# Order of high and low weight products, and the address of the high weights, in a hybrid decoder layer

## The chip, the cores and the metric

One core of one Trainium2 chip runs the whole program in one launch. The metric is device time in microseconds, from the start to the end of the execution, lower is better. The core has five instruction streams that run side by side and wait for each other by semaphores: TensorE (matmuls, PE in the profile, with PEld for the loads of its stationary operand), VectorE (DVE), ScalarE (ACT), GpSimd (POOL) and SyncE (SP, which here only issues DMAs).

## The reference

One decoder layer on 256 tokens of width 2048, in fp32. The weights are read once, 241 MB in all, and almost all the work lies in products of the 256 token rows with them:

```python
h = rms_norm(x, pre_mix_norm[l])
gq, gk, gv, gz, ga, gb, mq, mk, mv = jnp.split(h @ w_in[l], split_at, axis=-1)
y_gdn = gdn_branch(gq, gk, gv, gz, ga, gb, conv_w[l], a_log[l], dt_bias[l], gdn_norm_w[l])
y_moba = moba_branch(mq, mk, mv)
mix = jnp.concatenate([y_gdn, y_moba], axis=-1) @ w_out[l]
x = x + rms_norm(mix, post_mix_norm[l])
ca = memory_cross_attention(rms_norm(x, pre_mem_norm[l]), rms_norm(mem, mem_kv_norm[l]),
                            w_mq[l], w_mk[l], w_mv[l], w_mo[l])
x = x + rms_norm(ca, post_mem_norm[l])
f = jnp.square(jax.nn.relu(rms_norm(x, pre_mlp_norm[l]) @ w_up[l])) @ w_down[l]
x = x + rms_norm(f, post_mlp_norm[l])
```

`gdn_branch` is a gated delta rule over chunks with 8 heads, after a short convolution; `moba_branch` is causal softmax attention with 8 heads (at 256 tokens there is only the own block).

## The kernel before

**Three products for one.** TensorE works on operands of the type fp32r. To keep fp32's accuracy the kernel splits each operand into a high part, rounded to that type, and a low part, the rest. A product is then high x high + high x low + low x high, summed in one PSUM bank.

**The stream of weights.** `Stream` brings the weights in units of 128 x 1024 elements (128 x 512 for the first four), each by one DMA on SyncE's queue into a buffer `wraw` (5 of them). ScalarE casts it to `whi` (4 buffers) and VectorE subtracts to get `wlo` (4 buffers). `next()` hands out the next unit and issues those up to three ahead. `plan` lists the units in the order of use.

**Two kinds of products.** In the transposed ones (`a_tile`, `a_group`) the weights are the stationary operand and the tokens stream, so that the result has its features on the partitions. An activation tile holds high and low side by side (2 x 256 columns, `act[2][k]`), so the high weights take one matmul of 512 columns and the low weights one of 256 columns on the high half (`act[0][k]`). `a_tile` makes one tile of 128 features in 16 steps over the model width, two units of 8 steps; `a_group` makes four such tiles at once, in units of two steps by four tiles. `products` issues for each unit first its eight high matmuls and then its eight low ones (four and four in the first four units). In the other kind (`b_group`) the activation is stationary and the weights stream, 512 columns at a time, three matmuls for each step. Its last group in the cross-attention's output and in the layer's end splits the second of its two tiles into halves of 256 columns: for each unit six matmuls of 512 and then twelve of 256.

**The order of the work.** TensorE's order is that of the code (`manual_schedule`). After each unit `tick()` advances generators in the list `bg`, which hold the small work of the mixer and of the norms (transposes, Gram matrices, softmax); their matmuls stand between units. The other engines' order is made by the scheduler from the program's dependences; `pin` holds a few in place. Stages in time: the input projection with the mixer (activation `x`, to about 410 us), the output projection, the cross-attention (activations `m` and `h1`), and from about 597 us the MLP (activation `h`), twice half of the up projection (transposed) and half of the down projection (`b_group`, activations `f` and `fp`).

**Names in the rows.** `whi` and `wlo` are the high and low weights. `mm<-h,whi` is a matmul into a bank `mm` with moving `h` and stationary `whi`; `mm<-whi,fp` has the activation `fp` stationary. `wabh` are the high weights of the small gate projection (40 columns, slices of 160 bytes). Line 49 is `mm`, line 69 the cast, line 71 the subtraction. `mmb`, a broadcast row of the memory's norm, is the tile that changes its pool.

Of the kernel before, what the change touches and what calls it, by code (L numbers as in the profile page):

```python
# [7 lines left out]
F32 = mybir.dt.float32  # L8
F32R = mybir.dt.float32r
# [7 lines left out]
P = 128  # L17
T = 256
D = 2048
KT = 16  # L20
H = 8
HM = 4
# [6 lines left out]
NRAW, NHI, NLO, AHEAD = 5, 4, 4, 3  # L29
# [7 lines left out]
def layer(ctx, tc, x0, xT, xn, memT, cols, rows, wab, win, wout, wmq, wmk, wmv, wmo, wup, wdn, out):  # L37
# [4 lines left out]
    wp = ctx.enter_context(tc.tile_pool(name="wp", bufs=1))  # L42
    ap_ = ctx.enter_context(tc.tile_pool(name="act", bufs=1))
    sm = ctx.enter_context(tc.tile_pool(name="sm", bufs=1))
# [3 lines left out]
    def mm(o, l, r, start=True, stop=True, skip=False):  # L48
        TE.matmul(o, l, r, start=start, stop=stop, skip_group_check=skip)  # L49
# [3 lines left out]
    class Stream:  # L53


        def __init__(s, plan):
            s.units, s.done, s.pos, s.pin, s.ahead = [], [], 0, 0, AHEAD
            for n, (src, a, fine) in enumerate(plan):
                step = 1 if fine else a // 2
                s.units += [(n, src, a, k, step, fine) for k in range(0, a, step)]  # L60

        def emit(s):
            n, src, a, k, step, fine = s.units[len(s.done)]
            v = src.rearrange("p (a c) -> p a c", a=a)
            c = v.shape[2]
            r = wp.tile([P, step, c], F32, tag="wraw", name="wraw", bufs=NRAW)
            nc.sync.dma_start(r, v[:, k:k + step])
            hi = wp.tile([P, step, c], F32R, tag="whi", name="whi", bufs=NHI)
            cast = S.activation(hi, r, AF.Copy)  # L69
            lo = wp.tile([P, step, c], F32R, tag="wlo", name="wlo", bufs=NLO)  # L70
            sub = V.tensor_tensor(lo, r, hi.bitcast(F32), OP.subtract)  # L71
            if s.pin:
                s.pin -= 1
                pin(cast), pin(sub)
            s.done.append([(hi[:, i], lo[:, i]) for i in range(step)])
# [11 lines left out]
    def tick():  # L87
        for g in list(bg):
            if next(g, bg) is bg:
                bg.remove(g)  # L90
# [5 lines left out]
    def mmps():  # L96
        return ps.tile([P, 512], F32, tag="mm", name="mm", bufs=5)

    def aux():
        return ps.tile([P, 512], F32, tag="ax", name="ax", bufs=3)  # L100

    def products(steps):


        for o, w, act, k, first, last in steps:
            mm(o, w[0], act[2][k], start=first, stop=False)
        for o, w, act, k, first, last in steps:
            mm(o[:, :T], w[1], act[0][k], start=False, stop=last)

    def right(o):  # L110

# [4 lines left out]
    def a_tile(act):  # L116

        o = mmps()
        k = 0
        while k < KT:  # L120
            u = ws.next()
            products([(o, w, act, k + i, k + i == 0, k + i == KT - 1) for i, w in enumerate(u)])
            k += len(u)
            tick()
        return o

    def a_group(act, order, pre=None):

        o = [mmps() for _ in range(4)]
        n = 0  # L130
        while n < KT:
            u = ws.next()
            if pre:
                pre(n)
            cut = lambda w, c: [x[:, c * P:(c + 1) * P] for x in w]
            products([(o[c], cut(w, c), act, order[n + i], n + i == 0, n + i == KT - 1)
                      for i, w in enumerate(u) for c in range(4)])
            n += len(u)
            tick()
        return o  # L140

    def b_group(act, kts, last=False, banks=None):

        o = banks or [mmps() for _ in range(2)]
        whole = [[(b, slice(0, 512))] for b in o]
        if last:
            whole[1] = [(o[1][:, 0:T], slice(0, T)), (mmps()[:, 0:T], slice(T, 512))]

        def run(t, units, k):
            s = slice(t * P, (t + 1) * P)  # L150
            for b, c in whole[t]:
                for i, w in enumerate(units):
                    kt = kts[k + i]
                    f, l = k + i == 0, k + i == len(kts) - 1
                    mm(b, act[0][kt][:, s], w[0][:, c], start=f, stop=False)
                    mm(b, act[0][kt][:, s], w[1][:, c], start=False, stop=False)
                    mm(b, act[1][kt][:, s], w[0][:, c], start=False, stop=l)

        k = 0
        while k < len(kts):  # L160
            w = ws.next()
            while last and len(kts) - 8 <= k < len(kts) - len(w):
                w = w + ws.next()
            for t in range(2):
                run(t, w, k)
            k += len(w)
            tick()
        return whole
# [70 lines left out]
    def xslot(name):  # L239
        return parts(ap_.tile([P, KT, 2, T], F32R, tag="x", name=name))  # L240

    plan = [(win[i], 4, i == 0) for i in range(4)]
    for what, h in TURNS:
        i, n = {"mv": (24 + 4 * h, 4), "kq": (2 * h, 2), "m": (32 + 2 * h, 2), "v": (16 + h, 1), "z": (48 + h, 1)}[what]
        plan += [(win[i + j], 4 if what == "mv" else KT, False) for j in range(n)]
    plan += [(wout[i], 4, False) for i in range(16)]
    plan += [(wmk[i], KT, False) for i in range(HM)]
    plan += [(wmq[i], 4, False) for i in range(HM)]
    plan += [(wmv[i], 4, False) for i in range(4)]
    plan += [(wmo[i], 4, False) for i in range(4)]  # L250
    for half in range(2):
        plan += [(wup[32 * half + i], 4 if half == 0 and i < 4 else KT, False) for i in range(32)]
        plan += [(wdn[32 * half + i], 4, False) for i in range(32)]
    ws = Stream(plan)

    def scaled(dst, o, by, const=1.0):
# [12 lines left out]
    def prep(act, src, wcol, pool, k0, n, sq):  # L269
        xs = pool.tile([P, n, T], F32, tag="xs", name="xs", bufs=2 if n > 2 else 4)  # L270
        k1 = k0 % 4
        nc.sync.dma_start(xs, src[k0 // 4, :, k1:k1 + n])
        for k in range(n):
            norm_split(act, xs[:, k], wcol, k0 + k)
        S.activation(sq[:, k1:k1 + n], xs, AF.Square)

    def fold(sq):
        for n in (2, 1):
            V.tensor_tensor(sq[:, 0:n], sq[:, 0:n], sq[:, n:2 * n], OP.add)

    def col_sum(sq, name):

        pc = aux()
        for t in range(2):
            mm(pc[:, t:t + 1], sq[:, t * P:(t + 1) * P], ones[:, 0:1])
        return rstd_cols(pc[:, 0:2], name)
# [71 lines left out]
    with tc.tile_pool(name="p1", bufs=1) as p1:  # L358
        def t1(shape=None, name="t1"):
            return p1.tile(shape or [P, T], F32, tag="t1", name=name, bufs=14)  # L360
# [266 lines left out]
        mv = p1.tile([P, 2, 1024], F32, name="mv")  # L627
# [77 lines left out]
        for what, h in TURNS:  # L705
            if what == "mv":
                o = b_group(hx, list(range(KT)), banks=[mmps(), mmps() if h else aux()])
# [9 lines left out]
            if what == "m":  # L717
                q, k = t1(), t1()
# [6 lines left out]
            if what == "z":  # L725
                o = a_tile(hx)
# [6 lines left out]
        order = list(range(8, 15)) + list(range(8)) + [15]  # L733
# [6 lines left out]
    with ExitStack() as es:  # L740
        p2 = es.enter_context(tc.tile_pool(name="p2", bufs=1))
# [75 lines left out]
        ssm = []  # L817
        with tc.tile_pool(name="ld2", bufs=1) as ld2:
            def mem_in():
                acc = ld2.tile([P, 4, T], F32, name="macc")  # L820
                for q in range(4):
                    sq = ld2.tile([P, 4, T], F32, tag="msq", name="msq", bufs=2) if q else acc
                    prep(hm, memT, n_kv, ld2, 4 * q, 4, sq)
                    yield
                    if q:
                        V.tensor_tensor(acc, acc, sq, OP.add)
                    yield
                    yield
                fold(acc)
                for q in range(4):  # L830
                    nc.sync.dma_start(x1[:, 4 * q:4 * q + 4], xT[q])
                    yield
                yield
                ssm.append(col_sum(acc[:, 0], "mmr"))
                for _ in range(3):
                    yield
                ssm.append(sm.tile([P, T], F32, tag="mmb", name="mmb"))
                row_bcast(*ssm)

            bg.append(mem_in())  # L840
            late = list(range(12, 16)) + list(range(12))
            for c in range(4):
                om = b_group(y, order) if c else out_first
                stat_out(om, c, mix, lambda d, s: S.activation(d, s, AF.Copy))
            assert not bg
# [48 lines left out]
        o = b_group(hm, list(range(KT)), banks=[mmps(), aux()])  # L894
# [40 lines left out]
        for j in range(8):  # L935
            o = o_first[j] if j < 4 else a_tile(h2)
# [7 lines left out]
    for half in range(2):  # L944
# [11 lines left out]
        for c in range(4):  # L956
            o = b_group(f, list(range(32)), last=half == 1 and c == 3)
            cs = slice(512 * c, 512 * (c + 1))
# [14 lines left out]
    for t in range(2):  # L973
# [5 lines left out]
        for c in range(4):  # L979
            cs = slice(512 * c, 512 * (c + 1))  # L980
# [78 lines left out]
```

## Time and profile before

| | |
|---|---|
| runs (3) | median 1317.57 us, 1316.19 to 1318.88 |
| profiled execution | 1317.31 us, span of the core 1315.5 us |
| granted clock of TensorE, mean | 0.995 |
| TensorE busy with matmuls | 1295.0 us, 98% of the span, 6945 instructions |
| TensorE loading weights (beside the matmuls) | 1115.1 us, 85% |
| VectorE, ScalarE, GpSimd busy | 66%, 51%, 3% |
| DMA | 246 MB, mean 187 GB/s |

Busy time of TensorE is made of overlapping matmuls whose ends are modelled, so 98% says that it hardly ever stands still, not that it works at its peak. How fast it goes is read from the starts of its matmuls.

### The profile page before, as it was taken

The numbers are of one execution on the slowest core, as the hardware profiler recorded it, in microseconds if no ns is written. First come the engines' busy times: TensorE is split into PE (matmuls) and PEld (weight loads), VectorE is DVE, ScalarE is ACT, GpSimd is POOL, SyncE is SP. The second block draws the span as 40 slices with busy tenths as digits, with TensorE's granted clock in tenths as the row PEclk, the third lists the DMA queues.
The fourth block names the chain that finished last, engine by engine and source line by source line (L and its number), as shares of the span: only waits on it lengthen the run. The fifth ranks groups of instructions, "written<-read, shape, count | busy, mean of one in ns | idle before, by whom it ended". The sixth has DMA issues, their size and how long they took to land.

```text
span 1315.5 us, 18643 instructions
## 1 busy us (share of the span) xinstructions
PE 1295.0 (98%) x6945; PEld 1115.1 (85%) x6945; DVE 873.0 (66%) x1528; ACT 664.7 (51%) x1028; POOL 35.4 (3%) x64
## 2 busy tenths in 40 slices
PE   9999999999999999999999999999999999999997
PEld 8888888898887788888888888888888888888886
DVE  8988879867575759759966654444466666554555
ACT  7655544525555757657644444444444444443442
POOL 1010010100000000000000000000000000000000
PEclk9999999999999999999999999999999999999998
DMA  8655565624446865744665656666655565666662
GB/s 308 190 183 182 187 192 172 194 82 144 144 130 224 290 213 169 246 154 145 196 190 191 191 178 195 196 192 195 196 193 189 184 190 191 214 198 193 193 190 86
DMA packets 72378, 246.25 MB, mean 187 GB/s; under 512 B 10408, under 2 KB 11872, under 8 KB 71904
## 3 DMA queue, kind: packets, MB, share of 16 engines
q1 hardware_dynamic: 70016, 239.27, 56.3%
q0 software_dynamic: 2272, 5.80, 1.5%
q8 instruction: 54, 0.88, 0.3%
q14 instruction: 36, 0.29, 0.1%
HBM read 241.35 MB, written 3.69 MB: 186 GB/s over the span
## 4 chain that ended last, share of the span: by engine, by line
PE 66%; DMA 3%; DVE 2%; ACT 1%; issue 1%; DVEq 0%; SPq 0%; ACTq 0%; POOLq 0%
PE mm L49 63%; PE ax L49 2%; DMA xs<-in_memT_dram 2%; DMA t<-rd 1%; DMA wraw<-in_wout_dram 1%; DVE wlo L71 1%; PE ax L778 0%; DVE ca L981 0%; ACT whi L69 0%; DMA rd<-t 0%; ACT m L231 0%; PE ax L886 0%; DVE fd L965 0%; DVE yg L681 0%; ACT ca L772 0%
## 5 line engine op out<-in xcount | busy, mean ns | idle before, releaser
L71 DVE TENSOR_TENSOR wlo<-wraw,whi 128x1024 fp32r<-128x1024 f32 (+1 forms) x434 | 528.1, 1219 | 371.7 <-ACT whi L69 369.6
L69 ACT ACTIVATE whi<-wraw 128x1024 fp32r<-128x1024 f32 (+1 forms) x434 | 456.2, 1054 | 519.2 <-PE mm L49 341.4
L49 PE MATMUL mm<-h,whi 128*128 128x512 f32 x1024 | 256.8, 393 | 0.0
L49 PE MATMUL mm<-whi,fp 128*128 128x512 f32 (+1 forms) x816 | 240.3, 377 | 0.0
L49 PEld LDWEIGHTS mm<-h,whi 128*128 128x128 f32 x1024 | 184.2, 189 | 33.2 <-DVE h L232 0.2
L49 PE MATMUL mm<-x,whi 128*128 128x512 f32 x768 | 201.0, 404 | 1.1 <-ACT whi L69 1.1
L49 PEld LDWEIGHTS mm<-whi,fp 128*128 128x128 f32 x816 | 150.2, 188 | 28.1
L49 PEld LDWEIGHTS mm<-x,whi 128*128 128x128 f32 x768 | 140.7, 191 | 27.6 <-ACT whi L69 1.5
L49 PE MATMUL mm<-wlo,fp 128*128 128x512 f32 (+1 forms) x408 | 153.7, 377 | 0.0
L49 PEld LDWEIGHTS mm<-h,wlo 128*128 128x128 f32 x1024 | 139.7, 190 | 10.0
L49 PE MATMUL mm<-h,wlo 128*128 128x256 f32 x1024 | 142.8, 282 | 0.0
L49 PEld LDWEIGHTS mm<-x,wlo 128*128 128x128 f32 x768 | 105.2, 190 | 8.0
L49 PE MATMUL mm<-x,wlo 128*128 128x256 f32 x768 | 107.4, 282 | 0.0
L49 PEld LDWEIGHTS mm<-wlo,fp 128*128 128x128 f32 x408 | 76.8, 188 | 14.2
L49 PE MATMUL mm<-whi,f 128*128 128x512 f32 (+1 forms) x272 | 81.0, 377 | 0.0
L49 PEld LDWEIGHTS mm<-whi,f 128*128 128x128 f32 x272 | 50.1, 188 | 9.4
L49 PE MATMUL mm<-wlo,f 128*128 128x512 f32 (+1 forms) x136 | 51.3, 377 | 0.0
L113 ACT ACTIVATE right<-mm 128x256 f32<-128x256 f32 x120 | 44.9, 378 | 4.6 <-PE mm L49 2.5
L49 PE MATMUL mm<-whi,ym 128*128 128x512 f32 x128 | 42.5, 393 | 0.9 <-ACT whi L69 0.9
L49 PE MATMUL mm<-whi,yg 128*128 128x512 f32 x128 | 41.9, 391 | 0.4 <-ACT whi L69 0.4
L381 DVE SCALAR_TENSOR_TENSOR t<-xc,cl,t 128x256 f32<-128x256 f32 x72 | 34.6, 481 | 2.6 <-ACT t L379 1.5
L49 PE MATMUL mm<-whi,x 128*128 128x512 f32 x96 | 31.8, 396 | 0.0
(359 smaller groups left out, 1246.8 us busy)
## 6 DMA issues: line engine op xcount, KB each, us to landing
wraw<-in_wup_dram SPq DMA_DIRECT2D x128, 512.0 KB, 3.9
wraw<-in_wdn_dram SPq DMA_DIRECT2D x128, 512.0 KB, 4.4
wraw<-in_win_dram SPq DMA_DIRECT2D x110, 512.0 KB, 4.0
wraw<-in_wout_dram SPq DMA_DIRECT2D x32, 512.0 KB, 5.0
wraw<-in_wmk_dram SPq DMA_DIRECT2D x8, 512.0 KB, 4.5
wraw<-in_wmq_dram SPq DMA_DIRECT2D x8, 512.0 KB, 4.2
wraw<-in_wmv_dram SPq DMA_DIRECT2D x8, 512.0 KB, 5.1
wraw<-in_wmo_dram SPq DMA_DIRECT2D x8, 512.0 KB, 3.7
```

The source lines that it names most:

```text
L49: TE.matmul(o, l, r, start=start, stop=stop, skip_group_check=skip)
L69: cast = S.activation(hi, r, AF.Copy)
L71: sub = V.tensor_tensor(lo, r, hi.bitcast(F32), OP.subtract)
L113: S.activation(t, o[:, T:], AF.Copy)
L381: V.scalar_tensor_tensor(y, c[:, i:i + T], cw[:, 4 * ch + i:4 * ch + i + 1], y, OP.mult, OP.add)
```

## The change

The eight high and eight low matmuls of a unit no longer stand in two blocks: each high one is followed at once by its low one, in `a_tile` and in `a_group`. The tiles `whi` grow from 1024 to 1088 elements per partition. A unit that will be stationary is written 48 elements (192 bytes) into its buffer, one that will stream at the buffer's start. The 1 KB that this takes is given back by moving `mmb` from a pool that lasts all along to one that is opened later.

```diff
             for src, a, fine, off in plan:
                 step = 1 if fine else a // 2
-                s.units += [(n, src, a, k, step, fine) for k in range(0, a, step)]
+                s.units += [(src, a, k, step, off) for k in range(0, a, step)]
...
-            hi = wp.tile([P, step, c], F32R, tag="whi", name="whi", bufs=NHI)
+            hi = wp.tile([P, 1024 + 64], F32R, tag="whi", name="whi", bufs=NHI)
+            hi = hi[:, off:off + step * c].rearrange("p (a c) -> p a c", a=step)
             cast = S.activation(hi, r, AF.Copy)
...
-    def products(steps):
-
-
-        for o, w, act, k, first, last in steps:
-            mm(o, w[0], act[2][k], start=first, stop=False)
-        for o, w, act, k, first, last in steps:
-            mm(o[:, :T], w[1], act[0][k], start=False, stop=last)
+    def three(o, whi, wlo, act, k, first, last):
+
+        mm(o, whi, act[2][k], start=first, stop=False)
+        mm(o[:, :T], wlo, act[0][k], start=False, stop=last)
...
         while k < KT:
-            u = ws.next()
-            products([(o, w, act, k + i, k + i == 0, k + i == KT - 1) for i, w in enumerate(u)])
-            k += len(u)
+            for w in ws.next():
+                three(o, *w, act, k, k == 0, k == KT - 1)
+                k += 1
             tick()
...
-            products([(o[c], cut(w, c), act, order[n + i], n + i == 0, n + i == KT - 1)
-                      for i, w in enumerate(u) for c in range(4)])
-            n += len(u)
+            for w in u:
+                for c in range(4):
+                    cs = slice(c * P, (c + 1) * P)
+                    three(o[c], w[0][:, cs], w[1][:, cs], act, order[n], n == 0, n == KT - 1)
+                n += 1
...
-        plan += [(wup[32 * half + i], 4 if half == 0 and i < 4 else KT, False) for i in range(32)]
-        plan += [(wdn[32 * half + i], 4, False) for i in range(32)]
+        plan += [(wup[32 * half + i], 4 if half == 0 and i < 4 else KT, False, 48) for i in range(32)]
+        plan += [(wdn[32 * half + i], 4, False, 0) for i in range(32)]
...
-                ssm.append(sm.tile([P, T], F32, tag="mmb", name="mmb"))
+                ssm.append(p2.tile([P, T], F32, tag="mmb", name="mmb"))
```

The rest of `plan` gets its offsets in the same way: 48 for the input projection's transposed parts and for `wmk` and `wmq`, 0 for the values (`mv`), `wout`, `wmv` and `wmo`.

On TensorE, at the beginning of the MLP, the order before is this (`ca` is transposed for the norm, `h` is the normed activation):

```order
L778 MATMUL ax<-ident,ca 128x128 x16
L49 MATMUL mm<-h_6036,whi 128x512 x8
L49 MATMUL mm<-h_6036,wlo 128x256 x8
L778 MATMUL ax<-ident,ca 128x128 x4
L49 MATMUL mm<-h_6036,whi 128x512 x8
```

Of the change, at the same place, behind the transposes that stand between two units:

```order
L778 MATMUL ax<-ident,ca 128x128 x4
L49 MATMUL mm<-h_6036,whi 128x512
L49 MATMUL mm<-h_6036,wlo 128x256
L49 MATMUL mm<-h_6036,whi 128x512
L49 MATMUL mm<-h_6036,wlo 128x256
```

The blocks of eight are gone; the transposes stay where they were, between units. All transposed products change in this way, from the first instruction of the input projection on.

On ScalarE, early in the mixer, the order before is this (`right` is the copy of a bank's right half, `x0b` the broadcast norm):

```order
L69 ACTIVATE whi<-wraw 128x1024 x2
L113 ACTIVATE right<-mm 128x256 x2
L69 ACTIVATE whi<-wraw 128x1024 x4
L212 ACTIVATE x0b<-ax 128x256
L113 ACTIVATE right<-mm 128x256 x2
```

And of the change:

```order
L70 ACTIVATE whi<-wraw 128x1024 x3
L111 ACTIVATE right<-mm 128x256 x2
L70 ACTIVATE whi<-wraw 128x1024 x3
L211 ACTIVATE x0b<-ax 128x256
L111 ACTIVATE right<-mm 128x256 x2
```

One cast moved ahead of two copies. ScalarE's and VectorE's instructions change places by a few positions at some places up to the mixer's end, and stand as before behind it. Line numbers shift by one or two with the edit.

## Rows read from the trace of the kernel before

**Rows 1.** The page: busy time of TensorE; its granted clock in 40 slices.

```profile
PE 1295.0 (98%) x6945; PEld 1115.1 (85%) x6945; DVE 873.0 (66%) x1528; ACT 664.7 (51%) x1028; POOL 35.4 (3%) x64
...
PEclk9999999999999999999999999999999999999998
```

**Rows 2.** Groups of TensorE by shape: count, busy us, mean ns of one.

```profile
L49 PE MATMUL mm<-h,whi 128*128 128x512 f32 x1024 | 256.8, 393 | 0.0
...
L49 PE MATMUL mm<-x,whi 128*128 128x512 f32 x768 | 201.0, 404 | 1.1 <-ACT whi L69 1.1
L49 PE MATMUL mm<-h,wlo 128*128 128x256 f32 x1024 | 142.8, 282 | 0.0
...
L49 PE MATMUL ax<-x,wabh 128*40 128x256 f32 x32 | 5.7, 279 | 0.0
```

**Rows 3.** Timeline of TensorE in the MLP: start, length of the merged row, count.

```profile
701.89 2.00 PE L49 MATMUL mm<-h,whi 128*128 128x512 f32 x8
703.73 1.12 PE L49 MATMUL mm<-h,wlo 128*128 128x256 f32 x8
...
710.27 0.40 PE L49 MATMUL mm<-h,whi 128*128 128x512 f32 x1
```

**Rows 4.** Timeline of TensorE, activation-stationary products of the cross-attention's output.

```profile
580.77 0.39 PE L49 MATMUL mm<-wlo,chl 128*128 128x512 f32 x1
...
587.57 0.39 PE L49 MATMUL mm<-wlo,chl 128*128 128x512 f32 x1
...
588.50 0.28 PE L49 MATMUL mm<-wlo,chl 128*128 128x256 f32 x1
...
590.66 0.28 PE L49 MATMUL mm<-wlo,chl 128*128 128x256 f32 x1
```

**Rows 5.** Groups at 703.73 us: last high and first low matmul of a unit.

```profile
L49 PE MATMUL mm<-h,whi 128*128 128x512 f32 x1 | 0.4, 389 | 0.0
L49 PE MATMUL mm<-h,wlo 128*128 128x256 f32 x1 | 0.3, 278 | 0.0
```

**Rows 6.** Groups at 704.69 us: last two low and first high matmul.

```profile
L49 PE MATMUL mm<-h,wlo 128*128 128x256 f32 x2 | 0.4, 283 | 0.0
L49 PE MATMUL mm<-h,whi 128*128 128x512 f32 x1 | 0.4, 396 | 0.0
```

**Rows 7.** Timeline of TensorE, last product: two turns between 512 and 256 columns.

```profile
1286.34 0.40 PE L49 MATMUL mm<-wlo,fp 128*128 128x512 f32 x1
...
1291.98 0.40 PE L49 MATMUL mm<-wlo,fp 128*128 128x512 f32 x1
```

**Rows 8.** Timeline at the start: units five and six, TensorE and VectorE.

```profile
12.25 1.23 DVE L71 TENSOR_TENSOR wlo<-wraw,whi 128x1024 fp32r<-128x1024 f32 x1 [1.02 <-ACT whi L69]
12.27 2.11 PE L49 MATMUL mm<-x,whi 128*128 128x512 f32 x8 [0.72 <-ACT whi L69]
...
15.17 2.01 PE L49 MATMUL mm<-x,whi 128*128 128x512 f32 x8
...
15.59 1.22 DVE L71 TENSOR_TENSOR wlo<-wraw,whi 128x1024 fp32r<-128x1024 f32 x1
...
17.97 2.00 PE L49 MATMUL mm<-x,whi 128*128 128x512 f32 x8
```

**Rows 9.** Timeline at the beginning of the MLP: its second unit.

```profile
599.93 2.09 PE L49 MATMUL mm<-h,whi 128*128 128x512 f32 x8
600.55 2.35 DVE L71 TENSOR_TENSOR wlo<-wraw,whi 128x1024 fp32r<-128x1024 f32 x2
...
602.80 0.60 PE L778 MATMUL ax<-ident,ca 128*128 128x128 f32 x4
```

**Rows 10.** TensorE's waits: us in total, times, longest.

```profile
PE ax L49 <- DVE ym L660: 1.6, 1, 1.6
```

**Rows 11.** Timeline of ScalarE and VectorE in the MLP: one unit's cast and subtraction.

```profile
701.19 1.06 ACT L69 ACTIVATE whi<-wraw 128x1024 fp32r<-128x1024 f32 x1 [1.44 <-PE mm L49]
...
702.28 1.23 DVE L71 TENSOR_TENSOR wlo<-wraw,whi 128x1024 fp32r<-128x1024 f32 x1 [0.77 <-ACT whi L69]
```

More of the change, by code (lines that the diff above doesn't have):

```diff
@@ L57, in __init__ @@
             s.units, s.done, s.pos, s.pin, s.ahead = [], [], 0, 0, AHEAD
-            for n, (src, a, fine) in enumerate(plan):
+            for src, a, fine, off in plan:
                 step = 1 if fine else a // 2
-                s.units += [(n, src, a, k, step, fine) for k in range(0, a, step)]
+                s.units += [(src, a, k, step, off) for k in range(0, a, step)]
         def emit(s):
-            n, src, a, k, step, fine = s.units[len(s.done)]
+            src, a, k, step, off = s.units[len(s.done)]
             v = src.rearrange("p (a c) -> p a c", a=a)
@@ L134, in a_group @@
                 pre(n)
-            cut = lambda w, c: [x[:, c * P:(c + 1) * P] for x in w]
-            products([(o[c], cut(w, c), act, order[n + i], n + i == 0, n + i == KT - 1)
-                      for i, w in enumerate(u) for c in range(4)])
-            n += len(u)
+            for w in u:
[3 more added lines that the diff above has]
+                n += 1
             tick()
@@ L240, in xslot @@
         return parts(ap_.tile([P, KT, 2, T], F32R, tag="x", name=name))
-    plan = [(win[i], 4, i == 0) for i in range(4)]
+    plan = [(win[i], 4, i == 0, 48) for i in range(4)]
     for what, h in TURNS:
         i, n = {"mv": (24 + 4 * h, 4), "kq": (2 * h, 2), "m": (32 + 2 * h, 2), "v": (16 + h, 1), "z": (48 + h, 1)}[what]
[L245 to L250, printed above, removed]
+        plan += [(win[i + j], *((4, False, 0) if what == "mv" else (KT, False, 48))) for j in range(n)]
+    plan += [(wout[i], 4, False, 0) for i in range(16)]
+    plan += [(wmk[i], KT, False, 48) for i in range(HM)]
+    plan += [(wmq[i], 4, False, 48) for i in range(HM)]
+    plan += [(wmv[i], 4, False, 0) for i in range(4)]
+    plan += [(wmo[i], 4, False, 0) for i in range(4)]
     for half in range(2):
-        plan += [(wup[32 * half + i], 4 if half == 0 and i < 4 else KT, False) for i in range(32)]
-        plan += [(wdn[32 * half + i], 4, False) for i in range(32)]
+        plan += [(wup[32 * half + i], 4 if half == 0 and i < 4 else KT, False, 48) for i in range(32)]
+        plan += [(wdn[32 * half + i], 4, False, 0) for i in range(32)]
     ws = Stream(plan)
```

## The prediction

> **What bounds the kernel now.** I read the busy shares first. TensorE is busy for 98% of the span, at a granted clock of 90% or more of full, its 2.4 GHz level, in all slices but the last [rows 1], so the time is the sum of the spacings of its matmuls, and the other engines matter only where TensorE waits for them. By operation and shape, the matmuls that the change reorders come next: 512-column matmuls with high weights as stationary operand (1024 on h, 768 on x) and as many 256-column ones with low weights, 1024 of them on h [rows 2]. To these the program adds 64 and 64 for the memory's keys and the queries of the cross-attention (four tiles of 16 k-steps each), so 1920 pairs of one high and one low matmul change places. The products whose stationary operand is the activation keep their order.
>
> Lengths are not spacings, since matmuls overlap; spacings come from starts. In the MLP three units of eight pairs take from 701.89 to 710.27 us, 8.38 us or **349.2 ns per pair** [rows 3]. The unchanged products show what the same widths cost when they do not alternate: 30 matmuls of 512 columns in 6.80 us, 226.7 ns each, and 18 of 256 columns in 2.16 us, 120.0 ns each [rows 4]. A pair at these settled rates would take 346.7 ns. So a unit loses 8 x 2.5 = 20 ns above the settled rates. Where it loses them is seen in lengths: a settled 512 is 389 ns long, the first 256 behind it 278 [rows 5]; later 256s are 283 and the first 512 behind them 396 [rows 6]. Settled, 389 goes with 226.7 and 283 with 120.0, so a spacing is the length less about 162.7; hence 233.3 for a 512 just behind 256s, and 115.3 for a 256 just behind a 512. The same loss stands in a product with other operands at other addresses: the last one turns between six 512s and twelve 256s, and two such turns take 5.64 us [rows 7], 2.82 each, where settled rates give 6 x 226.7 + 12 x 120.0 = 2800 ns; 20 ns again. The loss thus belongs to turning from narrow to wide, not to an address or a tile.
>
> **The change, part by part.** Nothing is added to or taken from TensorE's work; the same matmuls stand in another order, with the same banks and sums. There are three parts.
>
> First, the alternation. Every low matmul now stands behind a wide one, and every high one behind a narrow one. For the low one the row is at hand: 278 ns, 115.3 apart, 4.7 below its settled spacing [rows 5]. For the high one there are two rows that disagree. A 512 whose successor is a low matmul, at the end of a group, is settled, 226.7 [rows 5]; a 512 directly behind narrow ones takes 233.3 [rows 6]. In the new order each high matmul is both. The narrow run ahead of it is now one matmul instead of eight, so I take the settled value. For the low one I do not take its best.
>
> Second, the shift by 192 bytes. It changes the address of the high weights against all other operands, and high weights are now loaded while a low matmul streams. No row shows this offset. The nearest is the small gate projection, whose stationary slices are 160 bytes apart and so lie at changing offsets to the moving tile: its 256-column matmuls are 279 ns long on average [rows 2], 116.3 apart, between the best (115.3) and the settled one (120.0). I take 116.3. A pair is then 226.7 + 116.3 = 343.0 ns, 6.2 less than now, and 1920 x 6.2 = **11.9 us** gained. Bounds for both parts together: if the shift takes from the high matmul also the 5 ns that separate 283 from 278, a pair is 221.7 + 115.3 = 337.0, 23.4 us gained; if it gives the low one nothing and the high one pays the turn, 233.3 + 120.0 = 353.3, 7.9 us lost.
>
> The Trainium skill speaks against this part. In "SBUF — State Buffer", section "Who interferes with whom", TensorE has two independent read ports, one for the moving operand and one for weight loads, and never waits on anyone. By it neither an offset nor the order of loads could move a spacing, and the gain here would be nothing; the trace disagrees so far that one and the same form is 278 or 283 ns long by its neighbours alone [rows 5, 6], but it does not show an offset as the cause.
>
> Third, waits. A unit's first low matmul now stands behind one high matmul instead of eight, so its low weights are wanted 7 x 230 ns = 1.6 us sooner, and VectorE makes them after ScalarE's cast. In the MLP that is covered: the cast for the unit four ahead starts as soon as the last high matmul of the present one has freed its buffer, and its low part is ready at 703.51 [rows 11], some 7 us before that unit starts at 710.27 [rows 3]. The buffer of high weights is now freed by the unit's second last matmul, about 0.8 us later, so of 7 us some 6 remain. Without that cover each unit would pay VectorE's 1.23 us. It is missing in two places. At the start the low weights come at 13.48 and 16.81 us while their high matmuls began at 12.27 and 15.17 [rows 8]: the first unit then ends at 13.48 + 0.12 + 7 x 0.343 = 16.0 and the next, from 16.81, at 19.33, against 17.97 now, 1.4 us later; the unit behind finds its weights ready. At the start of the MLP the second unit begins at 599.93 and its low weights are ready near 601.73 [rows 9], half of the two subtractions: it ends at 604.25 instead of 602.80, 1.5 us later. Together **2.9 us lost**. Both places keep ScalarE's and VectorE's order. SyncE's queue moves by single places only, and POOL's not at all.
>
> In the mixer, ScalarE's and VectorE's instructions change places by a few positions (a PSUM read and a cast, or the short-convolution steps and a subtraction). TensorE's waits there are single ones, the longest 1.6 us for the attention output [rows 10]; they can grow or shrink by as much, which I enter as 0 with 2 us on either side. The wider buffers cost 1 KB of space and no instruction; the moved broadcast tile costs none either.
>
> Sum, against the profiled execution (1317.3 us, its span 1315.5; the median of the runs is 1317.6): 1317.3 - 11.9 + 2.9 = **1308.3 us**.
>
> **The rivals.** *A: the settled rates hold, or the order does nothing for the rates.* The low matmul keeps 120.0 because the load under it, not its predecessor, sets it: 346.7 per pair, 4.8 gained, 2.9 lost, 1315.7. With no change of rate at all, 349.2, only the waits remain: 1320.2. Rows 4 speak for it, since 226.7 and 120.0 stand for tens of matmuls in a row; rows 5 against it. The second figure is what the skill's rule on the two ports gives. Chance 0.15, of which the rule has 0.05.
>
> *B: slower, since every high matmul pays the turn.* One unit has one turn from narrow to wide now and would have eight. If the price of the first slot (396, so 233.3 [rows 6]) falls on every high matmul while the low one stays at 120.0, a pair is 353.3 and the time 1317.3 + 7.9 + 2.9 = 1328.1; if the whole 20 ns came back each time, 366.7 per pair, 1353.8. What decides is the pair: above 349.0 ns, with the waits, the change is slower by over 0.2%. For it speaks that the 20 ns came twice from groups as unlike as 8 + 8 and 6 + 12 [rows 3, 7]; against it that most of the 20 falls on later slots of a wide run, which no longer exist, and that the first narrow one gives 4.7 back. Chance 0.17.
>
> *C: the shift removes more than I enter.* Pair 337 to 340, 1297 to 1303. The gate projection's mean is over several offsets [rows 2], so a chosen one can lie below it. Chance 0.26.
>
> **How the numbers follow.** The forecast has 0.42, A 0.15, B 0.17, C 0.26. A measurement tells 0.2% (2.6 us) from no change. Faster than that: the forecast and C, 0.68; A's first figure is within, 0.12 with a share of its second; slower 0.20. The likeliest gives 1308.3, alone 1304 to 1313 with the mixer's 2 us and half a nanosecond or more per pair either way. The range takes in most of C and all of A: 1299 to 1320, leaving out B and the far end of C.
>
> **What would show it.** In the profile after, the starts of one MLP unit give the pair: 343 if right, near 347 for A, above 349 for B, below 340 for C. The lengths say which half moved: high matmuls at 389 and low ones near 279. New idle time of TensorE behind the low weights' subtraction should stand at 13, 16 and 600 us and nowhere else in the units concerned; the activation-stationary products should keep 226.7, which would also show that moving the buffers did them nothing. Wrong would be: high matmuls at 396 throughout, waits for low weights in the mixer's units, or the 20 ns turning up again in the unchanged products.

## The result, and the profile after

| | before | changed |
|---|---|---|
| median of 4 runs each | 1317.92 us | 1302.43 us |
| range of the runs | 1316.19 to 1318.88 | 1301.81 to 1302.62 |
| profiled execution, span of the core | 1317.31, 1315.5 | 1302.26, 1300.5 |
| granted clock of TensorE, mean | 0.995 | 0.997 |

The changed kernel takes 0.9888 of the time before, 95% interval 0.9873 to 0.9903: 15.5 us faster, where the forecast of 1308.3 would be 9.6 below this median. What happened is rival C, at the upper end of its pair.

The page of the changed kernel: busy time by engine, the granted clock in 40 slices, and the groups by shape (count, busy us, mean ns of one, idle time before them).

```profile
PE 1278.4 (98%) x6945; PEld 1103.4 (85%) x6945; DVE 872.9 (67%) x1528; ACT 664.1 (51%) x1028; POOL 35.6 (3%) x64
...
PEclk9999999999999999999999999999999999999999
...
L49 PE MATMUL mm<-h,whi 128*128 128x512 f32 x1024 | 349.0, 390 | 0.0
L49 PE MATMUL mm<-h,wlo 128*128 128x256 f32 x1024 | 282.7, 276 | 0.0
...
L49 PE MATMUL mm<-x,whi 128*128 128x512 f32 x768 | 271.3, 398 | 0.4 <-ACT whi L70 0.3
...
L49 PE MATMUL mm<-x,wlo 128*128 128x256 f32 x768 | 213.4, 278 | 1.5 <-DVE wlo L72 1.5
```

As before [rows 1], TensorE hardly stands still, at its 2.4 GHz level, and it has the same 6945 matmuls. Busy sums can't be compared with [rows 2] here: a row that merges eight matmuls has their overlap taken out, and now nothing merges. The mean lengths can. On `h` the high matmul went from 393 to 390 ns and the low one from 282 to 276. On `x` the high one went from 404 to 398 only, and the low ones waited 1.5 us in all for their subtraction, all of it in the first 20 us.

The timeline of TensorE in the MLP of the changed kernel (start, length, operation) answers to [rows 3].

```profile
700.63 0.39 PE L49 MATMUL mm<-h,whi 128*128 128x512 f32 x1
700.86 0.28 PE L49 MATMUL mm<-h,wlo 128*128 128x256 f32 x1
...
703.01 0.39 PE L49 MATMUL mm<-h,whi 128*128 128x512 f32 x1
```

Seven pairs take 2.38 us, **340.0 ns per pair** instead of 349.2. The groups by shape of the same product, from 640 to 742 us, say which half moved:

```profile
L49 PE MATMUL mm<-h,whi 128*128 128x512 f32 x301 | 102.4, 389 | 0.0
L49 PE MATMUL mm<-h,wlo 128*128 128x256 f32 x301 | 83.1, 276 | 0.0
```

By the prediction's conversion (length less 162.7) these are 226.3 and 113.3 ns: the high matmul is settled throughout, and the low one is shorter than the 278 ns of the first narrow one of a block [rows 5], the best of the rows that the prediction had.

Not every pair has this rhythm. At the start, from 17.4 to 31.1 us, the timeline of the changed kernel shows another:

```profile
25.80 0.40 PE L49 MATMUL mm<-x,whi 128*128 128x512 f32 x1
26.04 0.28 PE L49 MATMUL mm<-x,wlo 128*128 128x256 f32 x1
...
28.25 0.40 PE L49 MATMUL mm<-x,whi 128*128 128x512 f32 x1
...
28.95 0.40 PE L49 MATMUL mm<-x,whi 128*128 128x512 f32 x1
```

Nine pairs take 3.15 us, 350 ns each, at the same offset and in the same order. Measured from each high matmul's start to the start of what follows its low one, 210 of the 1920 pairs take 343 to 354 ns: 178 of `x`'s 768 (349.4 on average), 17 of the cross-attention's 128 (346.4) and 15 of `h`'s 1024 (348.3). The longest runs of them are 39 pairs here at the start, and 31 from 205.7 us on, one pair behind four small matmuls of the mixer and without a wait.

The timeline at the start, of the changed kernel's unit five (answers to [rows 8]; the last bracket is the idle time before and what ended it):

```profile
12.58 1.23 DVE L72 TENSOR_TENSOR wlo<-wraw,whi 128x1024 fp32r<-128x1024 f32 x1 [0.88 <-ACT whi L70]
...
12.60 0.50 PE L49 MATMUL mm<-x,whi 128*128 128x512 f32 x1
...
13.86 0.38 PE L49 MATMUL mm<-x,wlo 128*128 128x256 f32 x1 [0.76 <-DVE wlo L72]
...
17.18 0.39 PE L49 MATMUL mm<-x,wlo 128*128 128x256 f32 x1 [0.33 <-DVE wlo L72]
```

The first low matmul of units five and six waits for the subtraction, as forecast; two waits of 0.22 us in the first two units, at 6.28 and 8.25 us, were not forecast. The tenth unit starts at 28.25 us (fence above), where steps of three units of 8.38 us from [rows 8]'s 17.97 put it at 26.35 before: 1.9 us lost. At the beginning of the MLP (answers to [rows 9]) the second unit looks like this:

```profile
594.09 0.48 PE L49 MATMUL mm<-h,whi 128*128 128x512 f32 x1
...
594.40 0.28 PE L49 MATMUL mm<-h,wlo 128*128 128x256 f32 x1
...
594.71 2.35 DVE L72 TENSOR_TENSOR wlo<-wraw,whi 128x1024 fp32r<-128x1024 f32 x2
```

The low matmul starts before the subtraction that the prediction took for its own: that one serves later units, and no wait stands here.

TensorE's waits (us in total, times, longest), of which [rows 10] is one row:

```profile
PE mm L49 <- DVE wlo L72: 2.9, 6, 0.8
...
PE ax L49 <- DVE t L260: 1.7, 2, 1.3
PE ax L49 <- ACT t L572: 1.6, 1, 1.6
...
PE ax L49 <- DVE ym L660: 0.7, 1, 0.7
```

The 2.9 us are 1.5 on `x` and 1.4 in the output projection, whose order did not change; before, the same row had 2.3 us, all of it there.

**The account.** 1920 pairs by 9.2 ns are 17.7 us. The 210 slower pairs keep back 1.9 of it (178 by 9.4 ns, the rest by 6 to 8 each), the start takes 1.9: 13.9 us. (The start's loss has its own pairs in it already, so the two items overlap by about 0.2 us.) The span is 15.0 shorter, so a little over 1 us came, net, from elsewhere. No single wait accounts for it: the wait for the attention output fell from 1.6 [rows 10] to 0.7, but the second `t` row above stood at 0.8 before and the first was not there. Set side by side matmul by matmul, single stretches of the mixer between 200 and 400 us differ by anything from 1.6 us lost to 1.8 gained. By stages: the MLP's first matmul stands at 590.83 us, 596.67 before, so 5.8 us were saved ahead of the MLP; from there to the end of the span 718.8 became 709.7, 9.1 us, against 1024 by 9.2 ns = 9.4. The unchanged last product still turns at its old price; its timeline in the changed kernel, answering to [rows 7]:

```profile
1265.66 0.40 PE L49 MATMUL mm<-wlo,fp 128*128 128x512 f32 x1
...
1271.30 0.40 PE L49 MATMUL mm<-wlo,fp 128*128 128x512 f32 x1
```

Two turns, 5.64 us, to the digit as before.

### The profile page after: what moved, and what is told of

Read it like the earlier page. It is cut to its first block, busy times and chain, and to the rows that moved or that the text cites. A ratio compares the mean times of both kernels' runs of the same rounds, so it can differ in the third digit from the quotient of the medians.

```text
span 1300.5 us, 18640 instructions
## 1 busy us (share of the span) xinstructions
PE 1278.4 (98%) x6945; PEld 1103.4 (85%) x6945; DVE 872.9 (67%) x1528; ACT 664.1 (51%) x1028; POOL 35.6 (3%) x64
## 4 chain that ended last, share of the span: by engine, by line
PE 87%; DVE 5%; DMA 4%; ACT 2%; issue 2%; SPq 0%; POOL 0%; DVEq 0%; ACTq 0%; POOLq 0%
PE mm L49 79%; PE ax L49 6%; DVE wlo L72 2%; DMA xs<-in_memT_dram 1%; ACT whi L70 1%; DMA wraw<-in_wout_dram 1%; DMA xr<-in_xn_dram 1%; DMA wrow<-in_rows_dram 1%; PE ax L778 0%; DMA t<-rd 0%; DMA xs<-in_xT_dram 0%; DVE ca L981 0%; DVE ntb L512 0%; DVE t L510 0%; DMA ccd<-t 0%
## 5 line engine op out<-in xcount | busy, mean ns | idle before, releaser
L72 DVE TENSOR_TENSOR wlo<-wraw,whi 128x1024 fp32r<-128x1024 f32 (+1 forms) x434 | 527.9, 1218 | 349.2 <-ACT whi L70 348.0
L49 PE MATMUL mm<-h,whi 128*128 128x512 f32 x1024 | 349.0, 390 | 0.0
L49 PE MATMUL mm<-h,wlo 128*128 128x256 f32 x1024 | 282.7, 276 | 0.0
L49 PE MATMUL mm<-x,whi 128*128 128x512 f32 x768 | 271.3, 398 | 0.4 <-ACT whi L70 0.3
L49 PEld LDWEIGHTS mm<-h,whi 128*128 128x128 f32 x1024 | 192.2, 188 | 39.8 <-DVE h L231 0.2
L49 PE MATMUL mm<-x,wlo 128*128 128x256 f32 x768 | 213.4, 278 | 1.5 <-DVE wlo L72 1.5
L49 PEld LDWEIGHTS mm<-h,wlo 128*128 128x128 f32 x1024 | 192.2, 188 | 0.0
L49 PEld LDWEIGHTS mm<-x,whi 128*128 128x128 f32 x768 | 144.3, 188 | 30.4 <-ACT whi L70 0.9
L49 PEld LDWEIGHTS mm<-x,wlo 128*128 128x128 f32 x768 | 144.3, 188 | 3.3 <-DVE wlo L72 2.8
```

## The experiments

The question was which part of the change makes 340 ns: the order, the address, or only both. The forecast had put most of the gain on the order (a low matmul behind a wide one is cheap whatever its address), the rest on the shift. All ratios are to the kernel before on the same chip, with 95% intervals; "pair" is the distance from one high matmul's start to the next, averaged in the MLP's two up projections, and two numbers are those of its first and its second half.

**Order alone.** Alternation and the wide buffers stay (1088 elements are 17 times 256 bytes), the offset becomes 0.

```diff
-    plan = [(win[i], 4, i == 0, 48) for i in range(4)]
+    plan = [(win[i], 4, i == 0, 0) for i in range(4)]
...
-        plan += [(wup[32 * half + i], 4 if half == 0 and i < 4 else KT, False, 48) for i in range(32)]
+        plan += [(wup[32 * half + i], 4 if half == 0 and i < 4 else KT, False, 0) for i in range(32)]
```

> The changed kernel with every unit written at the start of its wide buffer: alternation alone, without the 192 bytes. Theory 1 (the neighbour decides: a narrow matmul right behind a wide one is 113 ns apart, whatever the addresses) expects 1302 to 1304 us and pairs of 340 ns in the MLP, as with the change. Theory 2 (the offset does the work) expects no faster than before, 1316 to 1322 us, pairs of 347 ns or more. Theory 3 (a pair has two steady patterns, 340 and 350 ns, both of which stand in the trace of the change, and the offset picks the fast one) expects nearly all pairs at 350 and 1318 to 1321 us.

Measured: 1324.00 us against 1317.88, 1.0051 [1.0032, 1.0069], slower than before. Pair 353.3 in both halves. Timeline of TensorE in this kernel's MLP:

```profile
700.64 0.40 PE L49 MATMUL mm<-h,whi 128*128 128x512 f32 x1
700.88 0.28 PE L49 MATMUL mm<-h,wlo 128*128 128x256 f32 x1
700.99 0.40 PE L49 MATMUL mm<-h,whi 128*128 128x512 f32 x1
701.24 0.28 PE L49 MATMUL mm<-h,wlo 128*128 128x256 f32 x1
701.36 0.40 PE L49 MATMUL mm<-h,whi 128*128 128x512 f32 x1
701.59 0.28 PE L49 MATMUL mm<-h,wlo 128*128 128x256 f32 x1
701.70 0.40 PE L49 MATMUL mm<-h,whi 128*128 128x512 f32 x1
...
702.76 0.40 PE L49 MATMUL mm<-h,whi 128*128 128x512 f32 x1
```

Six pairs take 2.12 us, 353.3 each, and the spacings repeat after three pairs: high to low 0.24, 0.25, 0.23, low to high 0.11, 0.12, 0.11 us. The groups of this kernel from 640 to 742 us:

```profile
L49 PE MATMUL mm<-h,whi 128*128 128x512 f32 x290 | 102.5, 399 | 0.0
L49 PE MATMUL mm<-h,wlo 128*128 128x256 f32 x290 | 81.4, 281 | 0.0
```

High matmuls at 399, not 389: rival B's pair sum to the tenth, with the price on the high side, but not its split, which was 233.3 and 120.0; by the starts the high matmul takes 236.6 ns on average and the low one 116.8. Without the offset the alternation costs, so the neighbour alone does not make a pair cheap. Nor can the wider buffers or the moved broadcast tile be what gained, since this kernel has both.

**Address alone.** The offset stays, the order is the blocks of eight of before; `n = 8` here, other values below.

```diff
-    def three(o, whi, wlo, act, k, first, last):
-
-        mm(o, whi, act[2][k], start=first, stop=False)
-        mm(o[:, :T], wlo, act[0][k], start=False, stop=last)
+    def products(steps):
+        n = 8
+        for j in range(0, len(steps), n):
+            for o, w, act, k, first, last in steps[j:j + n]:
+                mm(o, w[0], act[2][k], start=first, stop=False)
+            for o, w, act, k, first, last in steps[j:j + n]:
+                mm(o[:, :T], w[1], act[0][k], start=False, stop=last)
...
```

> The offset alone: wide buffers and 192 bytes, but eight high and then eight low matmuls per unit, as before. Theory 1 expects the time of before within 2 us (1315 to 1319) and the pattern 396 to 389 and 278 to 283 ns in lengths. Theory 2 expects most of the gain, 1303 to 1308 us. Theory 3 expects the wide runs unchanged and at most the narrow ones a little nearer to 113 ns: 1310 to 1318 us.

Measured: 1315.73 us against 1317.88, 0.9986 [0.9973, 0.9999]. Pair 348.3 and 349.2, before 349.2 in both. Timeline in this kernel's MLP:

```profile
692.19 2.01 PE L49 MATMUL mm<-h,whi 128*128 128x512 f32 x8
694.03 1.10 PE L49 MATMUL mm<-h,wlo 128*128 128x256 f32 x8
694.97 2.01 PE L49 MATMUL mm<-h,whi 128*128 128x512 f32 x8
```

One unit takes 2.78 us, before 2.79. The address alone is worth at most a nanosecond per pair. So order alone moves the median by +6.1 us, the address alone by -2.2, both by -15.5: the gain belongs to the two together.

**Blocks of two** (`n = 2`, offset 192 bytes).

> Blocks of two high and two low matmuls, with the 192 bytes: four turns a unit in place of eight or one. If the first narrow matmul behind a wide one is the only one that is cheap (113 against 119 to 120 ns) and turns cost nothing, a pair is 343 ns and the time 1308 us. If each turn cost the 20 ns of before, a pair would be 357 ns and the time above 1330 us. If only strict alternation locks into the fast pattern, pairs are at 347 to 350 ns and the time 1315 to 1320 us.

Measured: 1318.83 us against 1317.88, 1.0012 [1.0000, 1.0023]. Pair 350.0, with low matmuls 116 and 120 ns and high ones 229 and 235 ns apart. Groups from 640 to 742 us:

```profile
L49 PE MATMUL mm<-h,whi 128*128 128x512 f32 x292 | 91.3, 394 | 0.0
L49 PE MATMUL mm<-h,wlo 128*128 128x256 f32 x292 | 57.8, 280 | 0.0
```

At this offset a step halfway to alternation gives nothing of the gain; of the three orders tried, blocks of eight, of two and strict alternation, only the last does.

**256 bytes instead of 192** (offset 64 elements).

> Alternation with 256 bytes in place of 192. If the offset counts modulo 256 bytes (all of the tiles concerned start at the same place modulo 256), this is the same as no offset: 1323 to 1326 us and MLP pairs of 353 ns. If any offset that parts the high weights from the rest does it, 1302 us and 340 ns.

Measured: 1324.22 us against 1315.79, 1.0062 [1.0047, 1.0077]; pair 353.3, high 399 and low 281 ns long, the same cycle of three pairs as with no offset. So the places below are given modulo 256 bytes; this is the one pair of offsets that tests it.

**64 bytes and 128 bytes** (offsets 16 and 32 elements).

> Alternation with 64 bytes. If any offset other than a multiple of 256 bytes does it: 1302 to 1304 us. If only some offsets do, somewhere between 1304 and 1324, with pairs of 343 to 353 ns; then the sign counts, since 192 bytes forward are 64 back.

> Alternation with 128 bytes, half of 256. If any offset but a multiple of 256 bytes does it: 1302 to 1304 us; if the distance from 192 counts, between the times of 64 and 192 bytes.

Measured with 64 bytes: 1312.72 us against 1315.79, 0.9980 [0.9970, 0.9991]. Groups of this kernel, first from 640 to 742 us, then from 990 to 1092 us, in the first and the second up projection:

```profile
L49 PE MATMUL mm<-h,whi 128*128 128x512 f32 x292 | 102.2, 394 | 0.0
L49 PE MATMUL mm<-h,wlo 128*128 128x256 f32 x292 | 82.1, 281 | 0.0
...
L49 PE MATMUL mm<-h,whi 128*128 128x512 f32 x301 | 102.4, 389 | 0.0
L49 PE MATMUL mm<-h,wlo 128*128 128x256 f32 x301 | 83.1, 276 | 0.0
```

The same instructions on the same buffers run at a mean of 350.0 ns all through the first half (most steps 348 to 352), and at 340 in 511 of 512 pairs of the second. With 128 bytes: 1320.96 us against 1315.79, 1.0036 [1.0022, 1.0051], pair 352.0 in both halves. The price is not monotone in the offset, and at 64 bytes it is not a function of the address alone: two rhythms exist, and each held for hundreds of pairs. The 350 ns pairs in the mixer of the changed kernel look like the same kind of thing at 192 bytes.

**Low weights shifted in the place of the high ones** (`wlo` gets the wide tile and the 192 bytes).

```diff
-            hi = wp.tile([P, 1024 + 64], F32R, tag="whi", name="whi", bufs=NHI)
-            hi = hi[:, off:off + step * c].rearrange("p (a c) -> p a c", a=step)
+            hi = wp.tile([P, step, c], F32R, tag="whi", name="whi", bufs=NHI)
...
-            lo = wp.tile([P, step, c], F32R, tag="wlo", name="wlo", bufs=NLO)
+            lo = wp.tile([P, 1024 + 64], F32R, tag="wlo", name="wlo", bufs=NLO)
+            lo = lo[:, off:off + step * c].rearrange("p (a c) -> p a c", a=step)
```

> Alternation with the low weights 192 bytes further in wide buffers, the high ones as before. If the parting of a weight load from the stream beside it counts for either load, 1302 to 1306 us and 340 ns per pair. If the load of the high weights under the narrow matmul is the one that suffers, as the 353 ns pairs with both at one place suggest (narrow ones at 113 to 120 ns), it stays at 1318 to 1325 us.

Measured: 1315.26 us against 1315.79, 0.9996 [0.9981, 1.0010]. Pair 346.7 in the first half, 350.0 in the second. Groups from 640 to 742 us:

```profile
L49 PE MATMUL mm<-h,whi 128*128 128x512 f32 x295 | 102.3, 396 | 0.0
L49 PE MATMUL mm<-h,wlo 128*128 128x256 f32 x295 | 81.9, 278 | 0.0
```

It is not the same which of the two lies further in.

**The activations moved instead.** A pad ahead of the activation buffers shifts what streams; in the first kernel by 64 bytes with both weights unshifted and the buffers not widened, so that against the streams both lie as the high ones do in the changed kernel, modulo 256 bytes; in the second by 192 bytes with the high weights at 128, so that against the streams the high ones lie at 192 and the low ones at 64.

```diff
...
+    ap_.tile([P, 16], F32, name="apad", tag="apad")
     hx = xslot("x0")
```

> Alternation with high and low weights at the same place modulo 256 bytes as before and without wider buffers, but all activation tiles 64 bytes further, so that both weight loads lie 192 bytes beyond the streams modulo 256. If what counts is each load against the stream beside it, the wide matmul runs as with the low weights alone moved (233 ns, low weights' load at 192 under it) and the narrow one at 113: pairs of 346 to 347 ns, 1313 to 1316 us. If what counts is high weights against low weights, it is as with none moved: 353 ns, 1323 us. If moving the high weights against the streams is enough, whatever the low ones do: 340 ns, 1302 us.

> Against the streams, modulo 256 bytes, the high weights lie at 192 as in the change, and the low weights at 64 in place of 0 (activations 192 bytes further, high weights 128). If only the high weights' place counts: pairs of 340 ns, 1302 us. If the low weights' place counts as well, the wide matmuls leave 227 ns: pairs of 345 to 350, 1311 to 1320 us. If a pair can go below 340 ns, this is where it might show.

Measured: the first 1333.70 us against 1316.78, 1.0134 [1.0104, 1.0164], pair 353.3; the second 1320.08 us, 1.0023 [1.0006, 1.0041], pair 353.3 and 346.7. In the first the activation-stationary products, which no kernel so far had moved, slowed too. Groups from 820 to 860 us of the changed kernel and, in the second fence, of this one:

```profile
L49 PE MATMUL mm<-whi,fp 128*128 128x512 f32 x96 | 29.7, 389 | 0.0
```

```profile
L49 PE MATMUL mm<-whi,fp 128*128 128x512 f32 x84 | 26.6, 396 | 0.0
L49 PE MATMUL mm<-wlo,fp 128*128 128x512 f32 x41 | 16.2, 396 | 0.0
```

389 is 226.3 ns by the conversion, 396 is 233.3: moving the stationary activation by 64 bytes costs about 7 ns per matmul, in an order that was not touched. The second kernel, with 192 bytes, slowed them too, by less: over all 512-column products on `f` and `fp` the starts are 228.9 ns apart, where they are 226.9 to 227.2 in the kernels with unmoved activations and 233.3 in the first. So the medians of these two kernels hold more than their pairs. With the changed kernel's place of the high weights against the stream, neither kernel gets its 340: the place of the high load against its stream does not decide by itself.

**The waits.** The changed order keeps blocks of eight in the first seven units and in the MLP's first two, so that the low weights are not wanted early there (`n = 8 if ws.pos <= 7 or 180 <= ws.pos <= 181 else 1`); in a second kernel in the first seven units only (`n = 8 if ws.pos <= 7 else 1`). The changed kernel ran again beside the second.

> The change, but the first seven units and the first two of the MLP in two blocks as before, so that the high matmuls cover the making of the low weights. If the new waits at the start cost what the trace of the change shows (its seventh unit begins 1.9 us later than before), it is 1.5 to 2 us faster than the change, 1300.5 to 1301; if something behind swallows that (a DMA or VectorE that is the limit there), the same as the change, 1302.4.

> The changed kernel itself, on the chip on which the next one runs, for a comparison within a fraction of a per cent: 1301 to 1304 us.

> The change with only the first seven units in two blocks as before (the MLP's units stay alternating, since the trace of the change shows no wait there). If the waits for low weights at the start reach the end of the run: 1.4 to 2 us below the changed kernel on the same chip. If a limit behind them takes it up (VectorE's work in the mixer, the DMA-bound stretch at the output projection): within 0.7 us of it.

Measured: the first 1301.01 us against 1317.88, 0.9874 [0.9856, 0.9893]; the changed kernel again 1301.80 against 1316.78, 0.9893 [0.9873, 0.9914]; the second 1300.46, 0.9885 [0.9862, 0.9907], span of its profile 1297.7 us against 1300.0 of the repeat. Timeline of TensorE in the second kernel:

```profile
18.57 2.01 PE L49 MATMUL mm<-x,whi 128*128 128x512 f32 x8
...
21.36 0.40 PE L49 MATMUL mm<-x,whi 128*128 128x512 f32 x1
...
21.71 0.39 PE L49 MATMUL mm<-x,whi 128*128 128x512 f32 x1
...
22.73 0.39 PE L49 MATMUL mm<-x,whi 128*128 128x512 f32 x1
```

After the blocks the first alternating pair takes 0.35 us, and the next three 1.02, 340 each: it goes straight into the good rhythm, where the trace above of the changed kernel spends 39 pairs in the slower one. But the cover need not be the cause. The repeat of the changed kernel has much the same waits, and its timeline is this:

```profile
16.94 0.38 PE L49 MATMUL mm<-x,wlo 128*128 128x256 f32 x1 [0.26 <-DVE wlo L72]
...
18.21 0.39 PE L49 MATMUL mm<-x,whi 128*128 128x512 f32 x1
...
20.25 0.39 PE L49 MATMUL mm<-x,whi 128*128 128x512 f32 x1
```

Six pairs take 2.04 us, 340 each: behind the wait in unit six one execution of the same kernel ran slow and the other fast. Behind the wait in unit five it was the other way round, 340 ns in the first trace and 350 in the repeat. The stretch of 31 slow pairs behind the mixer's small matmuls begins at 204 to 206 us in all four traces of this order and offset, covered or not. The second kernel's median is 1.3 us lower and is the lowest of all kernels run, but the intervals overlap, so the gain over the changed kernel is not told apart from none. Covering the MLP's second unit adds nothing that shows, as it must be where no wait stands.

## Why the prediction was right in its direction and too small

**High matmuls at 226.7: right.** 389 ns long in the MLP, but for the 15 slower pairs.

**Low matmuls at 116.3: this term was mis-sized.** They came at 113.3. Three ns by 1920 are 5.8 us, against a miss of 5.9 (1308.3 forecast, 1302.4 measured). That the two agree so well is luck: the slower pairs (1.9 lost), the smaller waits (1.0 gained) and the mixer (a little over 1 gained) happen to cancel. The row that set it, the gate projection's mean of 279 ns [rows 2], has offsets that change from slice to slice and no alternation; the lower bound of the range, 337.0 per pair, had room for it, and rival C named the reason.

**Behind the term, a step of the argument failed: that the neighbour makes the low matmul cheap and the shift only adds to it.** [Rows 5, 6] were read as "278 behind a wide one, whatever the address". With the order alone the pair was 353.3, with the address alone 348.3 to 349.2, with both 340.0: neither part has a price of its own that could be added to the other's. By the forecast's own choice (the high matmul settled, the low one no worse than settled) the order alone gave 346.7 at most. That the sum came near is luck in so far as both parts were changed together. The remark that the loss "belongs to turning from narrow to wide, not to an address or a tile" fell with it: [rows 3] and [rows 7] show the same 20 ns at the addresses that those two products have, but other addresses had not been seen. Rival B was right about the order: at offset 0 the change would have been slower, at B's first pair sum, 353.3. (Rival A's first time is 0.3 off its own terms: 1317.3 - 4.8 + 2.9 is 1315.4.)

**The two ports.** Kernels that differ in the offset alone ran at 353.3 (0 bytes), 340.0 (192) and 353.3 ns (256) per pair, at the same granted clock (0.996, 0.997 and 0.997), in stretches of the MLP where TensorE waits for no other engine. The rule of the Trainium skill, "SBUF — State Buffer", section "Who interferes with whom", that TensorE reads its moving operand and its weights through independent ports and never waits on anyone, gives the same time for all three; here the measurement decides against it, as far as TensorE's rate depends on where its weights lie. Whether one read gives way to the other, and which, or whether a read is slower at some places by itself, is not shown.

**Waits: the sum of 2.9 us was nearer 1.9, by two errors.** The start lost 1.9 instead of 1.4; 0.33 of the difference is that the fifth unit itself began later, at 12.60 instead of 12.27. The repeat of the changed kernel, with the good rhythm behind its waits, lost 1.4: its tenth unit began at 27.73. The MLP's second unit lost nothing instead of 1.5: the subtraction in [rows 9] was put down to the unit that ran at the time, where it was that of later units. Reading which unit a row serves would have needed the one before it.

**Mixer at 0 with 2 us either way: held**, a little over 1 us gained, as the net of single differences of up to 1.8 either way. **The MLP's cover: held**; no wait for low weights stands in its units. **Activation-stationary products at 226.7: held**, 389 long [rows 4]. The 20 ns in the unchanged last product, named as a sign of being wrong, stand there as before; they were in the time before too, so nothing in the sum hangs on them. What the prediction did not have is that a pair's rate depends on more than its order and addresses: 1.9 us of the gain stayed in the 210 slower pairs.

**What stays open** is the mechanism. In bytes modulo 256 against the streams, relative to before, (high, low) gave: (0, 0) 353.3; (64, 0) 350.0 or 340.0; (128, 0) 352.0; (192, 0) 340.0; (0, 192) 346.7 or 350.0; (192, 192) 353.3; (192, 64) 353.3 or 346.7. The place of the high weights alone does not decide: at 192 it gave 340.0, 353.3 and 346.7; nor does that of the low ones, at 0 from 340.0 to 353.3. The distance from low to high fits the ends of the list: 353.3 at distance 0 in all three kernels that had it (0, 256 bytes, and both weights at 192), 340.0 in the MLP at distance 192; but distances 64 and 128 gave three values each, and it says nothing of the activation-stationary products, which slowed without a pair of high and low weights to compare. How a rhythm is entered or left was seen, not explained. Nor is it shown that the place against the stream is what counts: in the kernel with both weights at 192 their own addresses are those of offset 0, and so is its pair, 353.3, so the weights' own place, or high against low, would fit that kernel as well. The writes of ScalarE and VectorE into the shifted tiles are a poor candidate: in the MLP of the changed kernel, from 604 us on, 478 pairs in a row keep 340 ns, while ScalarE is busy for 54% of the time up to 767 us and VectorE for 74%.

## What to carry to other kernels

Where TensorE never waits and its matmuls are at full clock, the spacing of their starts still has some per cent in it, and order and addresses set it together: try them as a grid (here four kernels: neither, each alone, both), since order alone made this one slower and the address alone did next to nothing. A price read from one address and one neighbour does not carry over to another pair of them. Look also at how a stretch begins: behind a wait or behind a few small matmuls TensorE ran in a slower rhythm for up to 39 pairs. Compare two executions of the same kernel before giving such a stretch a cause, since here the one had it behind a wait where the other had not.

## What the runs showed that was not expected

- Pairs of the same two matmuls settle at fixed means, 340.0, 346.7, 350.0, 352.0 and 353.3 ns, and hold them for hundreds of pairs; at 353.3 the pattern repeats after three pairs. No settled mean lay below 340.0.
- At one and the same offset (64 bytes) a product of 512 pairs ran at a mean of 350.0 throughout and another all but wholly at 340.
- Behind the same wait at the start, two executions of the changed kernel went into different rhythms, 350 and 340 ns.
- 256 bytes of shift are as good as none: 1324.22 and 1324.00 us.
- Moving the stationary activations by 64 bytes slowed 512-column matmuls in an unchanged order from 226.9 to 233.3 ns from start to start; by 192 bytes, to 228.9.
